# A mixture-of-experts kernel on one core: the head of x loaded by SyncE alone, in two pieces

## The chip, the cores and the metric

The kernel runs on one core of a Trainium2 chip. The core has five engines that run side by side and meet only through semaphores: TensorE (PE in the profile, PEld for its weight loads), VectorE (DVE), ScalarE (ACT), GpSimd (POOL) and SyncE (SP). Sixteen DMA engines move data between HBM and the on-chip memory (SBUF). A DMA is issued by SyncE, ScalarE or GpSimd; each of the three has a queue of its own on these sixteen engines: q1 is SyncE's, q10 ScalarE's, q0 GpSimd's. GpSimd's queue can also convert the data on the way, here from fp32 to bf16.

The metric is the device time of one execution in microseconds (us), the median of several runs. The span in a profile, from the first to the last instruction of the program, is a little shorter.

## The reference

Eight experts, each with its own 256 rows of x and its own two weight matrices:

```python
n_experts, capacity, hidden, expert_hidden = 8, 256, 512, 2048
h = np.matmul(x, w1)        # (8,256,512) x (8,512,2048)
h = np.maximum(h, 0)
out = np.matmul(h, w2)      # (8,256,2048) x (8,2048,512) -> (8,256,512)
```

Everything is fp32 in HBM. x has 4 MB, w1 and w2 have 32 MB each, and the output has 4 MB.

## The kernel before

**Layout.** x is seen as 128 partitions with R = 16 rows of 512 numbers each. w1 of an expert lies in SBUF as 128 partitions with all of its 2048 columns for K1 = 4 slices of the hidden dimension; w2 as 128 partitions with K2 = 16 slices. Both have NS = 4 slots, so expert e uses slot e mod 4. All weights become bf16 in the DMA.

**x comes in two parts.** The first HEAD = 6 of the 16 rows per partition come as fp32 into memory that belongs to the output (x_head, a part of out_sb), by two hardware-queue loads: rows 0 to 2 issued by SyncE and rows 3 to 5 issued by ScalarE (L137 to L141). Both raise the semaphore d_head. They are issued inside the Tile context; tc.close() and tc.compile() behind them (L142, L143) end that context with a barrier over all engines, and from there on the program is written by hand. The other ten rows are loaded by GpSimd behind that barrier (L158) straight into x_sb as bf16. x_sb is not memory of its own: it lies in slot 2 of w2_sb. VectorE waits for both head loads (d_head at 32) and casts the head to bf16 into x_sb in one instruction (L219).

**Transposes.** When the cast is done, the identity matrix is built and GpSimd's x load has landed, PE transposes x in 64 pieces of 128 by 128 (a loop over K1 = 4, 16 pieces each, matmuls recorded at the helper's line L280). VectorE and ScalarE copy the results from PSUM to xT (L211).

**Weights.** GpSimd issues twelve weight loads in one fixed order (L195): w1 then w2 for experts 0 and 1 together, then for 2 and 3, then w1 of 4 and 5, then w2 of 4, and so on, down to w2 of the last expert in two halves. Before some of them it waits until the slot is free: for w1 until the hidden matmuls of the expert four places earlier are done, for w2 until its output matmuls are. The load of w2 for experts 2 and 3 waits for all transposes, since x_sb lies in its place. q0 works these loads off in the order of issue.

**Who tells PE.** SyncE waits for each weight load to land, in that order (L148), and raises a counter that PE takes (helper `take`, L99). SyncE issues nothing else until the end, when it stores the last expert's output (L150).

**Compute.** Per expert PE makes 64 matmuls into h_ps in four groups; ScalarE applies the maximum with zero and writes hT (L244); then 32 matmuls into o_ps, which VectorE copies to out_sb (L230). The very last half is copied by ScalarE (L250). The outputs of the first seven experts go out in one large store by GpSimd (L198), queued behind the last weights.

Of the kernel before, what the change touches and what calls it, by code (L numbers as in the profile page):

```python
# [16 lines left out]
def kernel(  # L17
# [7 lines left out]
    nc = tc.nc  # L25
# [6 lines left out]

    R = E * C // P

    HEAD = 6

    NS = 4

# [94 lines left out]

    x_head = out_sb[:, :HEAD // MC].rearrange("p e m h -> p (e m h)")


    for queue, a, b in [(nc.sync, 0, HEAD // 2), (nc.scalar, HEAD // 2, HEAD)]:  # L137
        head = queue.dma_start(
            x_head[:, a * H:b * H], x_v[:, a * H:b * H]
        ).then_inc(d_head, 16)  # L140
        tc.info.no_tile_sem_insts.add(head.ins.name)  # L141
    tc.close()  # L142
    tc.compile()  # L143

    sp = nc.sync
    for i, (w, es, h, n) in enumerate(loads):
# [10 lines left out]
    pool = nc.gpsimd  # L157
    pool.dma_start(x_sb[:, HEAD * H:], x_v[:, HEAD * H:]).then_inc(d_pool, 16)  # L158
    pool.memset(identity[:], 0.0).then_inc(s_event)  # L159
# [58 lines left out]
    dve.wait_ge(d_head, 32)  # L218
    dve.tensor_copy(x_sb[:, :HEAD * H], x_head).then_inc(s_cast)  # L219
    dve.sem_inc(c_xt[0], 1)  # L220
# [259 lines left out]
```

## Time and profile before

| what | value |
|---|---|
| median of 3 runs | 179.18 us (179.18 to 179.47) |
| the profiled execution's own time | 179.18 us |
| its span | 177.9 us |
| busy share PE, ACT, DVE, POOL | 71%, 22%, 9%, 6% |
| share of the DMA engines' time by q0, q1, q10 | 97.1%, 2.1%, 1.1% |
| granted TensorE clock, mean | 0.942 |
| issue to landing of the head loads | 6.0 us (SyncE's), 6.9 us (ScalarE's) |
| issue to landing of GpSimd's x load | 10.5 us |

How to read the lines shown further down. In the busy line each digit is the busy share of one fortieth of the span in tenths. In a table of stretches each row gives the stretch, its length, the busy time and number of instructions of PE, PEld, DVE, ACT and POOL, the granted clock, the mean busy share of the DMA engines and the GB/s that they wrote; a packet counts where it starts, so shares of short stretches can pass 1. In the timeline a row gives start, duration, engine, line, operation, and in brackets how long the engine had been idle and what released it. "SPq" and the like are the engines' instruction queues, which handle semaphores and DMA issues.

### The profile page before, as it was taken

To read this page: it belongs to the slowest core of one execution; us is meant where nothing else is said; L and a number is where in the kernel's file an instruction comes from. 1 tells how busy PE (TensorE), PEld (TensorE's weight loads), DVE (VectorE), ACT (ScalarE), POOL (GpSimd) and SP (SyncE) were. 2 spreads that over 40 slices of the span, in tenths; PEclk is the share of its full clock that TensorE was granted. 3 is DMA by queue.
4 is the path that set the end of the run, shared out by engine and by line. 5 is a ranking of instruction groups with operands and counts; after the bars stand their busy time and mean duration, and the time that the engine had idled before them with its cause. 6 is when DMAs were issued, how large, how long until landed. Compare 5 with 4: busy or idle time off the path is not lost. (4 is left out here: it accounts for less than half of the span.)

```text
span 177.9 us, 2069 instructions
## 1 busy us (share of the span) xinstructions
PE 126.3 (71%) x824; PEld 89.5 (50%) x832; DVE 16.4 (9%) x20; ACT 38.7 (22%) x38; POOL 10.2 (6%) x21
## 2 busy tenths in 40 slices
PE   0008620794029999993059999999999999959980
PEld 0007510584014795692024794695596497449530
DVE  0214420000000200200000200200100020020010
ACT  2002420044000062054000062053044044006310
POOL 4300010000000002101000101100020000001000
PEclk9999999999558999999657999999999999999999
DMA  5999999989999989989999999999999999999998
GB/s 188 313 214 228 232 195 221 236 192 221 236 192 221 236 192 221 236 192 221 236 192 221 236 206 206 236 210 203 236 217 195 236 221 192 236 199 214 284 424 354
DMA packets 3888, 40.63 MB, mean 228 GB/s; under 512 B 304, under 2 KB 304, under 8 KB 1584
## 3 DMA queue, kind: packets, MB, share of 16 engines
q0 software_dynamic: 3456, 38.54, 97.1%
q1 hardware_dynamic: 288, 1.31, 2.1%
q10 hardware_dynamic: 144, 0.79, 1.1%
HBM read 71.30 MB, written 4.20 MB: 424 GB/s over the span
## 5 line engine op out<-in xcount | busy, mean ns | idle before, releaser
L280 PE MATMUL o_ps<-w_sb,hT 128*128 x248 | 59.7, 396 | 19.5 <-PEq L99 18.7
L280 PE MATMUL h_ps<-xT,w_sb 128*128 x512 | 60.7, 280 | 11.1 <-PEq L99 11.1
L280 PEld LDWEIGHTS h_ps<-xT,w_sb 128*128 x512 | 57.6, 145 | 15.1 <-issue 11.8
L244 ACT ACTIVATE hT<-h_ps 128x1024 bf16<-128x1024 f32 x32 | 32.8, 1024 | 109.6 <-PE h_ps L280 109.6
L280 PEld LDWEIGHTS o_ps<-w_sb,hT 128*128 128x128 bf16 x256 | 25.4, 101 | 51.1 <-issue 24.4
L230 DVE COPY out_sb<-o_ps 128x512 f32<-128x512 f32 x15 | 9.7, 687 | 139.7 <-PE o_ps L280 139.7
L280 PE MATMUL xt_ps<-identity,w_sb 128*128 128x128 bf16 x64 | 7.6, 310 | 15.7 <-PEq L99 15.7
L280 PEld LDWEIGHTS xt_ps<-identity,w_sb 128*128 x64 | 6.5, 144 | 16.5 <-issue 16.5
L195 POOL DMA_DIRECT2D w_sb<-in_w_dram x12 | 7.4, 616 | 104.4 <-PE h_ps L280 56.6
L211 ACT COPY xT<-xt_ps 128x1024 bf16<-128x1024 bf16 x4 | 4.0, 1012 | 17.0 <-PE xt_ps L280 17.0
L211 DVE COPY xT<-xt_ps 128x1024 bf16<-128x1024 bf16 x4 | 4.9, 1225 | 9.3 <-PE xt_ps L280 9.3
L198 POOL DMA_DIRECT2D out_dram<-out_sb x1 | 1.0, 964 | 33.0 <-DMA out_dram<-out_sb 33.0
L219 DVE CAST w_sb<-out_sb 128x3072 bf16<-128x3072 f32 x1 | 1.8, 1761 | 7.7 <-DMA out_sb<-in_x_dram 7.7
L250 ACT COPY out_sb<-o_ps 128x512 f32<-128x512 f32 x1 | 0.6, 586 | 5.9 <-PE o_ps L280 5.9
L211 ACT ACT_TABLE_LOAD x1 | 1.3, 1283 | 2.0 <-PEq L143 2.0
L186 POOL DMA_DIRECT2D out_dram<-out_sb x1 | 0.5, 512 | 14.7 <-DVEq L233 14.7
L158 POOL DMA_DIRECT2D w_sb<-in_x_dram x1 | 0.7, 682 | 2.0 <-POOLq L143 2.0
L162 POOL TENSOR_SCALAR_AFFINE_SELECT identity<-identity 128x128 bf16<-128x128 bf16 x1 | 0.3, 284 | 0.2 <-POOL identity L159 0.2
L159 POOL MEMSET identity<- 128x128 bf16 x1 | 0.2, 224 | 0.0
L464 POOL MEMSET const-float32-0.0<- 128x1 f32 x1 | 0.1, 93 | 0.2 <-issue 0.2
L464 POOL MEMSET const-bfloat16-1.0<- 128x1 bf16 x1 | 0.1, 96 | 0.0
L464 POOL MEMSET const-uint8-127<- 128x1 uint8 x1 | 0.1, 96 | 0.0
(1 smaller groups left out, 0.1 us busy)
## 6 DMA issues: line engine op xcount, KB each, us to landing
w_sb<-in_w_dram POOLq DMA_DIRECT2D x5, 4096.0 KB, 46.9
w_sb<-in_w_dram POOLq DMA_DIRECT2D x5, 2048.0 KB, 50.9
out_dram<-out_sb POOLq DMA_DIRECT2D x1, 3584.0 KB, 12.8
w_sb<-in_w_dram POOLq DMA_DIRECT2D x2, 1024.0 KB, 43.1
w_sb<-in_x_dram POOLq DMA_DIRECT2D x1, 1280.0 KB, 10.5
out_sb<-in_x_dram SPq DMA_DIRECT2D x1, 768.0 KB, 6.0
out_sb<-in_x_dram ACTq DMA_DIRECT2D x1, 768.0 KB, 6.9
out_dram<-out_sb SPq DMA_DIRECT2D x1, 512.0 KB, 4.6
```

Source lines behind the costliest of these rows:

```text
L158: pool.dma_start(x_sb[:, HEAD * H:], x_v[:, HEAD * H:]).then_inc(d_pool, 16)
L162: pool.affine_select(out=identity[:], in_=identity[:], compare_op=mybir.AluOpType.not_equal, fill=1.0, base=0, pattern=[[-1, P]], channel_ ...
L186: pool.dma_start(out_v[:16, 0, :16], out_sb[:16, 0, 0, :16]).then_inc(d_pool, 16)
L195: pool.dma_start(dst, src).then_inc(landed[i][0], 16)
L198: pool.dma_start(out_v[:, :E - 1, :], out_sb[:, :E - 1].rearrange("p e m h -> p e (m h)")).then_inc(d_pool, 16)
L211: return copy(xT[:, ko, m].rearrange("k (ep r2) -> k ep r2", r2=R // MC), xt_ps[m][:].rearrange("k r2 ep -> k ep r2"),)
L219: dve.tensor_copy(x_sb[:, :HEAD * H], x_head).then_inc(s_cast)
L230: cp = dve.tensor_copy(out_sb[:, e, m, :], o_ps[m][:])
L244: act.activation(hT[:, g * GJ:(g + 1) * GJ, :].rearrange("p a c -> p (a c)"), h_ps[g % UG][:], mybir.ActivationFunctionType.Relu,).then_in ...
L250: act.copy(out_sb[:, E - 1, 1, :], o_ps[1][:]).then_inc(v_last)
L280: return pe.add_instruction(inst)
L464: nc = _bacc.Bacc("TRN2", target_bir_lowering=False, num_devices=1)
```

## The change

Behind the change SyncE issues two loads for the head and ScalarE issues none. The first, four of the six rows, stands in the Tile context as before. The second, two rows, is SyncE's first instruction behind tc.close() and tc.compile(). Both raise d_head by 16, so the cast still waits for both (32). Rows, places in memory and everything behind them are unchanged.

```diff
-    HEAD = 6
+    FIRST, HEAD = 4, 6
...
-    for queue, a, b in [(nc.sync, 0, HEAD // 2), (nc.scalar, HEAD // 2, HEAD)]:
-        head = queue.dma_start(
+    def load_head(a, b):
+        return nc.sync.dma_start(
             x_head[:, a * H:b * H], x_v[:, a * H:b * H]
         ).then_inc(d_head, 16)
-        tc.info.no_tile_sem_insts.add(head.ins.name)
+
+    first = load_head(0, FIRST)
+    tc.info.no_tile_sem_insts.add(first.ins.name)
     tc.close()
     tc.compile()
+    load_head(FIRST, HEAD)
```

## The prediction

> **What bounds the kernel now.** First the whole profile: the busy line of the DMA engines, the queues' table, and the issues of the loads.
>
> ```profile
> span 177.9 us, 2069 instructions
> PE 126.3 (71%) x824; PEld 89.5 (50%) x832; DVE 16.4 (9%) x20; ACT 38.7 (22%) x38; POOL 10.2 (6%) x21
> ...
> DMA  5999999989999989989999999999999999999998
> q0 software_dynamic: 3456, 38.54, 97.1%
> q1 hardware_dynamic: 288, 1.31, 2.1%
> q10 hardware_dynamic: 144, 0.79, 1.1%
> HBM read 71.30 MB, written 4.20 MB: 424 GB/s over the span
> ```
>
> q0 is GpSimd's queue, q1 SyncE's, q10 ScalarE's. The digits stand at 8 or 9 in every slice but the first: the DMA engines have work from the second slice to the end, and 97.1% of their time goes to q0, the weights. PE, the busiest compute engine, has 71%. The profiled execution took 179.18 us, which is also the median of the three runs shown (179.18 to 179.47); 1.3 us of it lie around the span.
>
> Next the span cut into stretches. Columns: stretch, its length, busy time of PE, PEld, DVE, ACT and POOL, granted clock, DMA share, GB/s written.
>
> ```profile
> 1.50:3.00 1.50, 0.00 (x0) 0.00 (x0) 0.00 (x0) 1.02 (x1) 0.59 (x1) 1.00 0.78 152
> 3.00:6.00 3.00, 0.00 (x0) 0.00 (x0) 0.00 (x0) 0.27 (x1) 2.61 (x6) 1.00 1.01 422
> 6.00:12.50 6.50, 0.00 (x0) 0.00 (x0) 1.76 (x1) 0.00 (x0) 0.17 (x1) 1.00 1.14 247
> 12.50:32.40 19.90, 7.57 (x64) 6.52 (x64) 4.90 (x4) 4.05 (x4) 0.72 (x1) 1.00 1.00 213
> 32.40:51.80 19.40, 9.69 (x64) 8.33 (x65) 0.00 (x0) 4.10 (x4) 0.00 (x0) 0.81 1.01 216
> 90.50:158.20 67.70, 65.47 (x411) 44.09 (x416) 6.44 (x10) 16.39 (x16) 2.65 (x5) 0.96 1.01 216
> 167.90:175.50 7.60, 4.66 (x22) 1.91 (x20) 0.69 (x1) 0.59 (x1) 0.00 (x0) 1.00 1.03 423
> ```
>
> From 3 us on the DMA share is 1.00 or more. The written rate drops to about 215 GB/s only because the weights shrink from four bytes to two on the way: that is some 430 GB/s read, close to the 422 of the head. So nothing of the front part of the kernel has a price of its own except a moment in which the DMA engines stand still; whatever the order of the loads in the first 12.5 us, the same bytes pass before the first weights.
>
> The chain that ended last says how the end hangs on this stream, and the timeline shows the waits that it meets (in brackets the idle time before an instruction and what ended it).
>
> ```profile
> 158.30 7.31 PE h_ps L280 x64
> 172.60 0.59 ACT out_sb L250
> ```
>
> ```profile
> 32.46 0.83 PE L280 MATMUL h_ps<-xT,w_sb 128*128 x3 [9.20 <-PEq L99]
> 158.30 7.31 PE L280 MATMUL h_ps<-xT,w_sb 128*128 x64 [1.88 <-PEq L99]
> 173.21 0.35 SPq L150 DMA_DIRECT2D out_dram<-out_sb  x1
> ```
>
> L99 is the helper that takes a counter, here the one that SyncE raises when weights land: the last expert's w1 lands at 158.2, and PE, ScalarE and the last store follow. The other stores share the engines with it at 423 GB/s. A stream that is later by some time makes the end later by the same time, and PE's start at 32.46 waits for weights too.
>
> **The change part by part.** The pieces it touches:
>
> ```profile
> 0.74 0.38 SPq L138 DMA_DIRECT2D out_sb<-in_x_dram  x1
> 0.74 0.39 ACTq L138 DMA_DIRECT2D out_sb<-in_x_dram  x1
> 1.98 1.28 ACT L211 ACT_TABLE_LOAD   x1 [1.98 <-PEq L143]
> 2.40 0.68 POOL L158 DMA_DIRECT2D w_sb<-in_x_dram  x1 [1.96 <-POOLq L143]
> L143 SPq DRAIN  x3: 7/7/129, 1.2 to 1.6; - x3
> L143 ACTq DRAIN  x2: 8/81/154, 1.2 to 1.6; - x2
> L143 SPq EVENT_SEMAPHORE  x2: 17/17/17, 1.5 to 1.8; - x2
> ```
>
> *ScalarE's load goes* (0.39 us of issue). It stands ahead of the closing barrier of the Tile context (L143), which lets GpSimd go at 1.96. But SyncE's issue stands there too, started at the same 0.74 and took 0.38, and it stays; its first drain (129 ns at most against ScalarE's 154) ends 0.03 us before ScalarE's at best. So the barrier opens at most 0.03 us sooner. ScalarE's own work gains nothing: behind its table load it waits for PE's transposes, which start at 13.49 (row below). And even GpSimd's x load at 2.40 is queued behind the head's bytes, as the queues' table of the first 6 us shows:
>
> ```profile
> q1 hardware_dynamic: 128, 0.78, 40.9%
> q10 hardware_dynamic: 116, 0.71, 29.3%
> ```
>
> No packet of q0 moved before 6.0, although GpSimd's instruction was over at 3.1. Cost: 0.
>
> *SyncE's first load has four rows in place of three* (1024 KB in place of 768). Same issue count, same 0.38; the packets of a partition's rows get longer and not more. Cost 0 on the issue side.
>
> *SyncE's second load* (two rows, 512 KB) is one more issue on SyncE, 0.38 us, right behind the barrier's last semaphore on SP (1.8). What is queued behind it is the wait for the first weights, over at
>
> ```profile
> L148 SPq EVENT_SEMAPHORE  x2: 17/17/17, 32.3 to 51.7; - x2
> ```
>
> so 30 us cover it. When can its bytes flow? The first load's: the stretch 1.50:3.00 cut in 40 pieces of 0.0375 us, with its queues:
>
> ```profile
> GB/s 0 0 0 0 0 0 164 492 328 328 164 328 492 0 0 0 0 0 0 0 164 164 328 0 0 0 328 164 164 0 164 164 164 0 492 492 492 164 164 164
> q1 hardware_dynamic: 21, 0.13, 59.8%
> q10 hardware_dynamic: 16, 0.10, 18.5%
> ```
>
> The first piece with bytes is the seventh, at 1.73: 1.0 us behind the issue at 0.74. The second load, issued at about 1.85, is then ready at 2.85. The first load is done later: 0.23 MB by 3.0 (152 GB/s x 1.5 us), the rest of its 1.049 MB at 422 GB/s takes 1.94 us, so 4.94. Two us of margin, no hole. Then 0.524 MB at 422 take 1.24: the head's bytes end at 6.18. Today: 1.573 MB, (1.573 - 0.228) / 0.422 = 3.19, so 6.19. Cost 0.
>
> *What is late if the two rows mix with GpSimd's x load.* Both may then wait in their queues at 4.9. At worst the two rows end with that load, at 12.5 in place of 6.2, and land about 1 us later. The cast of the head (1.76 us at 7.68 now, in the 6.00:12.50 row) then ends at about 15.3, and the transposes, which start at
>
> ```profile
> 13.49 1.89 PE L280 MATMUL xt_ps<-identity,w_sb 128*128 128x128 bf16 x16 [13.49 <-PEq L99]
> ```
>
> slip by 1.8 us. PE's 9.20 us of idle time ahead of 32.46 cover this. GpSimd's w2 load that waits for the transposes,
>
> ```profile
> 3.98 2.18 POOL L195 DMA_DIRECT2D w_sb<-in_w_dram  x3 [0.15 <-issue]
> ...
> 23.56 0.72 POOL L195 DMA_DIRECT2D w_sb<-in_w_dram  x1 [17.39 <-PE xt_ps L280]
> ```
>
> goes out at 25.4 in place of 23.56. Three weight loads stand ahead of it on q0 since 3.98, and the second of them lands only at 51.7, so q0 stays full. Cost 0; it would begin to cost only when the transposes slipped by more than PE's idle 9.20.
>
> *One ring where there were two, while the stream starts up.* This the trace does not show. The stretch 1.50:3.00 carried 0.23 MB where 422 GB/s would have carried 0.63: 0.40 MB, or 0.96 us, are lost in the start-up. Lower end: all of that regained, -0.96, which the first piece's position already excludes in part (0.23 us pass before any byte): -0.7. Upper end: q1 carries no more than its own 0.13 MB there, and q10's 0.10 MB is missing: +0.24. The nearest row for one hardware queue alone is the last store:
>
> ```profile
> 176.20:177.20 1.00, 0.00 (x0) 0.00 (x0) 0.00 (x0) 0.00 (x0) 0.00 (x0) 1.00 0.95 389
> q1 hardware_dynamic: 99, 0.39, 94.6%
> ```
>
> In this microsecond q1, all but alone, kept the engines 95% busy: one ring is enough. I take 0.
>
> Sum: 179.18 + 0 (ScalarE's issue) + 0 (longer first load) + 0 (second load, covered by 2.1 us of bytes) + 0 (late cast, covered by 9.20) + 0 (start-up) = **179.2 us**.
>
> **The rivals.** *Slower: a hole behind the first load.* If SyncE's second load gets no bytes moving until the first has landed, and GpSimd's x load is truly not ready before 6.0 (no q0 packet is seen earlier), the DMA engines stand idle from 4.94 to 6.0, and the stream is late by 1.06 us: 179.18 + 1.06 = 180.2. It decides from the point where both are later than 4.94. For it: no row of before has two loads back to back on SyncE's queue. Against: twelve weight loads follow one another on q0 at a share of 1.00 to 1.01 without a hole, the x load's instruction was over at 3.1, and q0's packets begin just where the head's end, as those of a queue do that has been waiting. The Trainium skill speaks for this rival: its page "DMA: Bandwidth & Descriptors", section "Anatomy of one DMA — SWDGE (gpsimd) path", fits each DMA with about 2.0 us fixed plus its bytes at 436 GB/s, mostly for the receipt of the last byte. Paid in line behind the first load, that would make an estimate of 181.2. The trace of before does not agree on q0: where the next load is already queued, the share stays at 1.00 to 1.01 across the landings.
>
> *Faster: the start-up shrinks.* If the two rings hinder one another at the start (between 1.99 and 2.25 no packet starts, then both queues do), one ring could fill the engines earlier. Half of the 0.96 us regained gives 179.18 - 0.48 = 178.7. For it: that gap. Against: the gap can as well be the first packets' own way to HBM, which one ring has too.
>
> *Another null: the rows mix with the x load*, worked out above: same 179.2, but a later cast.
>
> **How the numbers follow.** No change, by either order, has 0.53: its own range is 178.9 to 179.5, the spread of the runs shown. The hole has 0.19 (179.6 to 180.2), the shorter start-up 0.16 (178.5 to 178.8); a start-up slower by up to 0.24 and what no row shows have the other 0.12, of which 0.06 stays within 0.2% (0.36 us, about what a measurement of this kernel can tell from no change), 0.04 is slower and 0.02 faster. Faster 0.18, same 0.59, slower 0.23. The range 178.6 to 180.2 holds the null, the hole up to its full price and most of the faster case, whose bound of -0.7 it leaves out.
>
> **What would show it.** Right: no q10 in the queues' table; q1 with about 1.57 MB in the first 6.2 us and a DMA share of about 1.0 over 3.0 to 6.0; the transposes within 2 us of 13.49; PE's first hidden matmul at 32.4 to 32.5 and the last expert's at 158.3. A hole shows as a share clearly under 1.0 between 4.9 and 6.0, with 158.3 moved by as much. A shorter start-up shows as more than 152 GB/s in 1.50:3.00, and both times earlier. The prediction is wrong if w1 of the last expert lands more than 0.4 us from 158.2, or if the time outside the span, 1.3 us, changes with ScalarE's queue gone, which no row can tell.

## The result, and the profile after

The changed kernel takes 180.23 us (median of 6 runs, 180.01 to 180.86) against 179.18 us of the kernel before (6 runs, 179.07 to 179.47). The ratio is 1.0059, with a 95% interval of 1.0046 to 1.0072: slower by 0.6%. The profiled execution took 180.51 us, 1.33 more than that of before, and its span grew by 1.3.

The page of the changed kernel, its lines of the span, the queues, the loads of x and the last store (KB and us from issue to landing):

```profile
span 179.2 us, 2069 instructions
...
q0 software_dynamic: 3456, 38.54, 96.6%
q1 hardware_dynamic: 432, 2.10, 3.2%
...
w_sb<-in_x_dram POOLq DMA_DIRECT2D x1, 1280.0 KB, 12.0
out_sb<-in_x_dram SPq DMA_DIRECT2D x1, 1024.0 KB, 4.7
out_sb<-in_x_dram SPq DMA_DIRECT2D x1, 512.0 KB, 12.3
out_dram<-out_sb SPq DMA_DIRECT2D x1, 512.0 KB, 3.0
```

q10 is gone and q1 carries all of the head. GpSimd's x load, untouched by the change, takes 12.0 us to land in place of 10.5. The second head load takes 12.3.

The timeline of the changed kernel:

```profile
0.74 1.49 SPq L137 DMA_DIRECT2D out_sb<-in_x_dram  x2
2.40 0.68 POOL L160 DMA_DIRECT2D w_sb<-in_x_dram  x1 [1.96 <-POOLq L144]
14.25 1.76 DVE L221 CAST w_sb<-out_sb 128x3072 bf16<-128x3072 f32 x1 [14.25 <-DMA out_sb<-in_x_dram]
16.46 1.89 PE L282 MATMUL xt_ps<-identity,w_sb 128*128 128x128 bf16 x16 [16.46 <-PEq L99]
26.54 0.72 POOL L197 DMA_DIRECT2D w_sb<-in_w_dram  x1 [20.37 <-PE xt_ps L282]
33.75 2.54 PE L282 MATMUL h_ps<-xT,w_sb 128*128 x11 [7.51 <-PEq L99]
159.62 2.75 PE L282 MATMUL h_ps<-xT,w_sb 128*128 x12 [2.67 <-PEq L99]
```

The first row joins both of SyncE's issues; it ends at 2.23, and the second began at 1.90. For the cast the kernel before had this row:

```profile
7.68 1.76 DVE L219 CAST w_sb<-out_sb 128x3072 bf16<-128x3072 f32 x1 [7.68 <-DMA out_sb<-in_x_dram]
```

The barrier opens when it did: GpSimd issues its x load at 2.40 in both. The cast moves from 7.68 to 14.25, the transposes from 13.49 to 16.46, and PE still sits idle for 7.51 us behind them before the first weights are there. But the weights are late: PE starts on them at 33.75 in place of 32.46, and on the last expert's at 159.62 in place of 158.30. The 1.3 us arise before the first weights have landed and stay the same to the end.

The stretches of the changed kernel, with the columns of the table shown for before:

```profile
1.50:3.00 1.50, 0.00 (x0) 0.00 (x0) 0.00 (x0) 1.02 (x1) 0.60 (x1) 1.00 0.78 202
3.00:6.00 3.00, 0.00 (x0) 0.00 (x0) 0.00 (x0) 0.26 (x1) 2.61 (x6) 1.00 1.02 388
6.00:12.50 6.50, 0.00 (x0) 0.00 (x0) 0.00 (x0) 0.00 (x0) 0.17 (x1) 1.00 1.04 214
158.20:167.90 9.70, 8.28 (x60) 7.42 (x61) 0.00 (x0) 3.07 (x3) 0.96 (x1) 0.82 1.01 213
```

The start-up is better than before (202 GB/s against 152). Then 3.00:6.00 moves 388 in place of 422, and 6.00:12.50 moves 214 in place of 247, with a DMA share of 1.0 all the time. There is no hole. The engines are busy and move less: single packets take longer, as the packet records of the next section show.

The same records show which engine counts. The 16 engines finish their parts of the first weights between 31.43 and 31.92 in the kernel before, and between 32.00 and 33.27 in the changed one: 0.62 us later on average, 1.35 for the last. In all twenty profiles of this document the span ends 145.9 to 146.0 us behind that last engine (146.2 in head4_only). So the time follows the slowest engine at the first weights.

The chain that ended last, for the end:

```profile
159.62 8.93 PE h_ps L282 x64
175.54 0.58 ACT out_sb L252
```

PE needs 8.93 us for the last hidden matmuls in place of 7.31, at a granted clock of 0.82 in 158.20:167.90. That is not what the change costs. The last store is issued later, but lands in 3.0 us in place of 4.6, and the span grows by the same 1.3 us that the weights are late. Two of the kernels below show the same pair without a difference in time: in sp4_sp2_inside the clock of this stretch is 0.82 and the last store takes 3.1 us, in sp4_act2_inside 1.00 and 4.6, and the span of both is 177.7.

### The profile page after: what moved, and what is told of

The parts are those of the page before. It is cut to its first block, busy times and chain, and to the rows that moved or that the text cites. A ratio compares the mean times of both kernels' runs of the same rounds, so it can differ in the third digit from the quotient of the medians.

```text
span 179.2 us, 2069 instructions
## 1 busy us (share of the span) xinstructions
PE 126.6 (71%) x824; PEld 89.6 (50%) x832; DVE 16.4 (9%) x20; ACT 38.7 (22%) x38; POOL 10.2 (6%) x21
## 5 line engine op out<-in xcount | busy, mean ns | idle before, releaser
L282 PE MATMUL h_ps<-xT,w_sb 128*128 x512 | 61.4, 282 | 10.2 <-PEq L99 10.2
## 6 DMA issues: line engine op xcount, KB each, us to landing
out_dram<-out_sb POOLq DMA_DIRECT2D x1, 3584.0 KB, 12.9
out_sb<-in_x_dram SPq DMA_DIRECT2D x1, 512.0 KB, 12.3
```

Source lines behind the costliest of these rows:

```text
L282: return pe.add_instruction(inst)
```

## The experiments

Each changes something about how the loads are issued. In the cuts of their code `...` stands for lines left out. Where load_head has four arguments, the first is the engine that issues, and True marks a load that stands in the Tile context. "First weights" is SyncE's first wait for a landing; it stands at 32.3 us in the kernel before and at 33.6 in the changed kernel:

```profile
L150 SPq EVENT_SEMAPHORE  x12: 17/17/17, 33.6 to 169.2; - x12
```

### Place, ring or sizes

Three things change together: the second load's place (behind the closing), its ring, that is, the queue (SyncE's twice), and the sizes (four and two rows). Four kernels set them apart.

```diff
 # sp4_sp2_inside: both of SyncE's loads in the Tile context
+    load_head(nc.sync, 0, FIRST, True)
+    load_head(nc.sync, FIRST, HEAD, True)
     tc.close()
     tc.compile()
-    load_head(FIRST, HEAD)
...
```

> Both of SyncE's loads stand in the Tile context, so the second is issued some 0.8 us sooner; sizes and ring are those of the changed kernel. Theory P (the place behind the closing makes the second load late on some DMA engines, GpSimd's x load cuts in there, and the slowest engine sets when the first weights land): 179.2 us, first weights landed at about 32.3, head landed before 8. Theory R (two loads in one ring do it): 180.2, first weights at 33.6. Theory S (loads of 4 and 2 rows, with 8 KB and 4 KB pieces, do it): 180.2.

Measured: 179.08 us, ratio 0.9987 [0.9976, 0.9999], first weights at 32.1.

```diff
 # sp4_act2_inside
+    load_head(nc.sync, 0, FIRST, True)
+    load_head(nc.scalar, FIRST, HEAD, True)
     tc.close()
     tc.compile()
-    load_head(FIRST, HEAD)
...
```

> The kernel before with 4 rows on SyncE and 2 on ScalarE, both in the Tile context: the sizes alone. Theory S: 180.2 us, first weights landed at 33.6. Theories P and R: 179.2 and 32.3.

Measured: 179.14 us, ratio 0.9992 [0.9980, 1.0005], first weights at 32.1. The sizes cost nothing.

```diff
 # sp4_act2_behind
...
     tc.compile()
-    load_head(FIRST, HEAD)
+    load_head(nc.scalar, FIRST, HEAD, False)
```

> 4 rows on SyncE in the Tile context, 2 rows on ScalarE behind the closing: the place and the sizes of the changed kernel, but two rings. Theories P and S: 180.2 us, first weights landed at 33.6, head landed at about 14. Theory R: 179.2 and 32.3, head landed before 8.

Measured: 180.43 us, ratio 1.0070 [1.0053, 1.0087], first weights at 33.4, cast at 13.30. Two rings do not help.

```diff
 # sp3_sp3_behind
-    first = load_head(0, FIRST)
+    load_head(nc.sync, 0, HEAD // 2, True)
     tc.close()
     tc.compile()
-    load_head(FIRST, HEAD)
+    load_head(nc.sync, HEAD // 2, HEAD, False)
...
```

> SyncE loads three rows in the Tile context and three behind the closing: place and ring of the changed kernel, sizes of the kernel before. Theories P and R: 180.2 us or more, since the first load is shorter and ends at about 4.3 us. Theory S: 179.2.

Measured: 181.05 us, ratio 1.0088 [1.0063, 1.0113], first weights at 34.2. So neither the ring nor the sizes alone cost anything; the three slow kernels share the place behind the closing, where the second load is issued at 1.9 us (inside, SyncE issues it at 1.17). Sizes matter in that a shorter first load makes it worse. With both loads inside, the barrier also opens later (GpSimd issues its x load at 2.88 in place of 2.40); that this is not what helps is shown further down, by pool_x_later, where a later x load does not help, and by sp5_sp1_behind, which is clean with the x load at 2.41.

The kernel with both loads inside has the sizes and the ring of the changed kernel, so the two can be laid side by side, but for its x load, issued 0.48 us later. What the queues carried from 4.8 to 6.0 us and from 6.5 to 8.5 us (packets, MB, share of the 16 engines' time), first with both loads inside:

```profile
DMA packets 136, 0.53 MB, mean 439 GB/s; under 512 B 13, under 2 KB 13, under 8 KB 132
q1 hardware_dynamic: 133, 0.50, 100.8%
...
DMA packets 45, 0.46 MB, mean 230 GB/s; under 512 B 0, under 2 KB 0, under 8 KB 0
q0 software_dynamic: 45, 0.46, 109.4%
```

and in the changed kernel:

```profile
DMA packets 113, 0.42 MB, mean 348 GB/s; under 512 B 14, under 2 KB 14, under 8 KB 111
q1 hardware_dynamic: 111, 0.40, 95.8%
...
DMA packets 39, 0.35 MB, mean 175 GB/s; under 512 B 0, under 2 KB 0, under 8 KB 8
q0 software_dynamic: 31, 0.32, 88.1%
q1 hardware_dynamic: 8, 0.03, 4.3%
```

In the first stretch the busy time is nearly the same, with a fifth fewer bytes; in the second, 31 packets of the x load start in place of 45. In the packet records a 4 KB piece of the second load takes 0.16 us, but five of them near 5 us take 0.3 to 1.1; a piece of the x load takes 0.77 us, but many near 7 us take 1.0 to 1.2. Added up over the 16 engines, the packets that are more than 0.1 us too long account for 0.60 us per engine, 0.16 of it in the second load and 0.45 in the x load, and the bytes moved up to 14 us are 0.62 us behind those of before. With both loads inside the same count gives 0.01.

Not every engine is hit alike. Twelve of the 16 finish the second load at 6.1 to 6.3 us, the other four, on which it shares the engine with the x load, at 10.8 to 13.9. A load has landed when the last of the 16 engines has: GpSimd's x load, issued at 2.40, lands at 2.40 + 12.0 = 14.4 in place of 2.40 + 10.5 = 12.9. So the mean is 0.62 us late and the first weights 1.3.

### GpSimd's descriptors, or a load into a running stream

```diff
 # pool_x_later: a fill of 128x1024 fp32 in an unused part of out_sb first
...
+    pool.memset(out_sb[:, E - 1], 0.0).then_inc(s_late)
+    pool.wait_ge(s_late, 1)
     pool.dma_start(x_sb[:, HEAD * H:], ...)
...
 # pool_w_later: three such fills ahead of the weight loads
```

> The changed kernel, but GpSimd first fills a part of out_sb that nobody reads before it is overwritten (estimated at 1.1 us from the 0.22 us for 128 columns), so that its x load and its weight loads are issued about 1.1 us later. Theory G (SyncE's second load is held up because GpSimd writes the descriptors of its own loads at the same time): the second load of the head gets through, the head's bytes end near 6.2, first weights land near 32.3, 179.2 us, unless the x load itself now comes too late. Theory B (a hardware-queue load that is issued while the DMA engines already move data comes through slowly, whoever else issues): the stream is disturbed between 4.9 and 8 us as in the changed kernel, 180.2 us.

Measured: 180.32 us, ratio 1.0063 [1.0046, 1.0080], first weights at 33.5. The x load was issued at 3.17. Here the head landed early (cast at 7.50), and now it is the x load's first packets that are stretched, by up to 1.1 us each. The loss is as large, but it has moved to the other load. So the second load gets through as theory G had it, and the time is as theory B had it.

> The changed kernel, but GpSimd makes three such fills between the identity and the first weight load, so that the x load stays where it was and the three weight loads are issued near 7 us in place of 4 to 6.2. Theory G in the form that the weight loads' descriptors do it: undisturbed from 4.9 to 6.5 and about 179.2 us. Theory G in the form that the x load's descriptors (2.4 to 3.1 us) do it, and theory B: 180.2.

Measured: 180.10 us, ratio 1.0053 [1.0037, 1.0070], first weights at 33.2, with the weight loads issued from 7.05 on. Their descriptors have no part in it.

```diff
 # head4_only: no second load, GpSimd loads twelve rows
-    FIRST, HEAD = 4, 6
+    HEAD = 4
...
-    load_head(FIRST, HEAD)
...
-    dve.wait_ge(d_head, 32)
+    dve.wait_ge(d_head, 16)
```

> The second load is left out: SyncE loads four rows in the Tile context, GpSimd the other twelve (1536 KB). If the disturbance belongs to the second hardware-queue load, this is as fast as before or a little faster, 179.0 to 179.2 us, with q0's first packets at about 4.9. If GpSimd's x load is itself not ready before 6 us, a hole from 4.9 to 6 shows and the time is about 180.2.

Measured: 180.14 us, ratio 1.0057 [1.0040, 1.0074], first weights at 32.6. What q0 and q1 carried from 4.4 to 6.0 us:

```profile
q0 software_dynamic: 30, 0.37, 113.6%
q1 hardware_dynamic: 31, 0.12, 18.7%
```

q0 starts as soon as the four rows are through (first packet at 4.7), so GpSimd's x load is ready long before the 6.0 at which it is first seen in the kernel before. Packets are stretched by 0.10 us per engine, less than in the changed kernel, although the x load is only 2.3 us old when it starts. The first weights are only 0.3 us late, yet the runs are 1.0 us slower, of which the profiled execution, the fastest of the four (179.73), shows 0.55; where the rest lies in the others isn't known. Neither of the two forecasts holds: there is no hole, and leaving the second load out does not bring the time of before back.

```diff
 # both_behind: both of SyncE's loads behind the closing
-    first = load_head(0, FIRST)
     tc.close()
     tc.compile()
+    load_head(0, FIRST)
     load_head(FIRST, HEAD)
```

> Both of SyncE's loads stand behind the closing, one right after the other (about 1.9 and 2.3 us), so that the stream starts about 1.16 us later than in the kernel before, which costs 1.16 by itself: 180.3. Theory B: the second is issued before the DMA engines move data, so nothing is added: 180.3, and the stretch in which the head moves runs at about 420 GB/s. Theory G: the second load is generated beside GpSimd's x load, the stream is disturbed as well: 181 or more.

Measured: 179.79 us, ratio 1.0032 [1.0020, 1.0043], first weights at 32.9. With no DMA to issue, the closing itself is over sooner (loads at 1.39 and 1.82), so the start is late by 0.65 us and not by the 1.16 that was expected; 0.40 us of that is left by 4 us, and the stream loses only 0.15 more. The second load's first packet is at 5.3, 3.5 us behind its issue. Stretches of this kernel:

```profile
3.50:6.00 2.50, 0.00 (x0) 0.00 (x0) 0.00 (x0) 0.00 (x0) 2.16 (x3) 1.00 1.09 427
```

427 GB/s: as theory B has it, no disturbance worth the name.

```diff
 # pool_x_after_head
+    pool.wait_ge(d_head, 32)
     pool.dma_start(x_sb[:, HEAD * H:], ...)
```

> The changed kernel, but GpSimd issues its x load only when the whole head has landed, so that the second load has the DMA engines for itself and a hole opens between the head and the x load. The time itself is of no use (about 182 us with a hole of some 2 to 3 us). Theory B (a hardware-queue load issued while data already moves is held up by itself): the head's last bytes move at clearly less than 420 GB/s and the second load lands later than 7.6. Theory M (it is the meeting of the second load with the x load on the engines): the second load moves at about 420 GB/s, ends at 6.2 and lands at about 7.2, and the x load behind it is undisturbed too.

Measured: 183.5 us in one run, with the hole that was expected. The second load alone on the engines still has five stretched packets (0.3 to 0.5 us), but lands by 7.15. The x load behind the hole:

```profile
7.43 1.60 POOL L161 DMA_DIRECT2D w_sb<-in_x_dram  x1 [6.98 <-DMA out_sb<-in_x_dram]
DMA packets 16, 0.16 MB, mean 109 GB/s; under 512 B 0, under 2 KB 0, under 8 KB 0
```

The second line is for 9.5 to 11.0 us: one packet per engine in that time, stretched by 0.4 to 1.0 us, starting 2.3 us behind the beginning of the issue, which itself took 1.60 us here in place of 0.68. Neither theory said this: a load that starts on idle engines is slow in its first packets, on q0 here as on q1 at the kernel's start, where the first sixteen 8 KB pieces take 0.4 to 1.05 us each and later ones 0.31.

```diff
 # before_plus_early, before_plus_late: the kernel before and a third load
     sp = nc.sync
...
+    sp.wait_ge(d_head, 32)          # only in before_plus_late
+    sp.dma_start(out_sb[:, 4]..., x_v[:, 4 * H:6 * H]).then_inc(d_extra, 16)
...
+                dve.wait_ge(d_extra, 16)   # before VectorE writes there
```

> The kernel before plus a third load: SyncE reads two rows of x once more, behind the closing, into a part of out_sb that is not yet in use (VectorE waits for it before it writes there). Its 0.524 MB cost 1.24 us at 422 GB/s. Theories B and M: on top of that the x load is stretched and the first weights land later by about 1 us: 181.2 or more, first weights at 34.5. If only a load that the cast waits for matters: 180.4, first weights at 33.5.

Measured: 180.54 us, ratio 1.0073 [1.0054, 1.0092], first weights at 33.6, 1.3 us later: the price of the bytes and no more. Behind the start-up not one packet is stretched, though the load was issued at 1.90 into a running stream, as in the changed kernel; its own first packet is at 6.0, 4.1 us behind the issue. Theory B falls in its general form, and so does M.

> The same third load, but issued when the head has landed (about 7.7 us), into the middle of GpSimd's x load. 1.24 us for its bytes. Theory B in its general form (any hardware-queue load issued into a running stream disturbs it): about 1 us on top, first weights at 34.5, 181.4 us. If the disturbance belongs to the meeting of two loads that both have just been issued: 180.4, first weights at 33.5.

Measured: 180.49 us, ratio 1.0071 [1.0054, 1.0087], first weights at 33.6. Again only the bytes.

```diff
 # sp6_inside: all six rows in one load
-    FIRST, HEAD = 4, 6
+    HEAD = 6
...
-    load_head(FIRST, HEAD)
...
-    dve.wait_ge(d_head, 32)
+    dve.wait_ge(d_head, 16)
```

> All six rows in one load by SyncE in the Tile context, none by ScalarE. No load is issued behind the closing on a hardware queue, so by every theory left this is undisturbed: 179.0 to 179.2 us, first weights at 32.1 to 32.3.

Measured: 179.09 us, ratio 0.9995 [0.9985, 1.0005], first weights at 32.3, and behind the start-up only three packets are more than 0.1 us too long (by 0.12 at most). ScalarE's load is not needed, and taking it away brings nothing.

### How old a load is when its turn comes

What the clean runs with a load in the Tile context share is that the bytes issued there last longer. That can be tried directly.

```diff
 # sp5_sp1_behind: FIRST, HEAD = 5, 6     sp2_sp4_behind: FIRST, HEAD = 2, 6
 # sp6_sp2_behind: FIRST, HEAD = 6, 8 (GpSimd loads eight rows)
 # sp6_sp2_later: the same, and
+    nc.sync.wait_ge(s_event, 2)     # GpSimd's identity
     load_head(FIRST, HEAD)
```

> Five rows in the Tile context, one row behind the closing. The first load's bytes end at about 5.5 us, so the second, issued at 1.9, has a lead of 3.6. Theory L (the lead counts, 3.6 us are enough): 179.1 to 179.3 us, first weights landed at 32.2 to 32.4. Theory A (0.63 us per row of the second load): 179.8, 32.9.

Measured: 179.45 us, ratio 1.0014 [0.9999, 1.0030], first weights at 32.2. One packet of the second load is 0.19 us too long, none of the x load.

> Six rows in the Tile context and two behind the closing (8 rows by SyncE, 8 by GpSimd). The second load is the one of the changed kernel in size and time of issue, but its turn comes at about 6.1 us, a lead of 4.2. Theory L: 179.1 to 179.3 us, first weights at 32.2 to 32.4. Theory A: 180.4, 33.6.

Measured: 179.20 us, ratio 1.0003 [0.9992, 1.0014], first weights at 32.2, no packet of the second load or of the x load stretched. This is the second load of the changed kernel, same size, same place, same issue at 1.90. Its turn comes later, and GpSimd has eight rows in place of ten. Theory A (a price per row) falls.

> As sp6_sp2_behind, but SyncE issues the second load only when GpSimd's identity is finished (about 3.9 us), so that its lead is 2.2 us. Theory L: disturbed again, as much as the kernel with three rows and three rows, first weights at 33.6 to 34.2, 180.4 to 181. Theory A: as sp6_sp2_behind. If the cover of x load and weights already queued on GpSimd's queue fills in, it is clean: 179.2.

Measured: 179.22 us, ratio 1.0001 [0.9992, 1.0011], first weights at 32.3, the third of the cases named; theory L's own forecast (33.6 to 34.2) missed. The x load was ready and went first, and the two rows came in between its packets from 7.4 us on, when they were 3.5 us old and not 2.2:

```profile
0.74 3.44 SPq L137 DMA_DIRECT2D out_sb<-in_x_dram  x2
15.40 2.29 DVE L222 CAST w_sb<-out_sb 128x4096 bf16<-128x4096 f32 x1 [15.40 <-DMA out_sb<-in_x_dram]
```

(The first row joins both issues: the second ends at 4.18.) The cast is later here than in the changed kernel, and it costs nothing.

> Two rows in the Tile context and four behind the closing; the first load's bytes end at about 3.6 us, a lead of 1.7. Theory L: the worst of the row, first weights later than 34.2 and more than 181 us. Theory A: four rows at 0.63, 34.8 and 181.7.

Measured: 181.72 us, ratio 1.0144 [1.0126, 1.0162], first weights at 34.7, the worst of the row as both theories said.

The kernels in one row, by the age of the second load (the time since its issue, the lead of the expectations) when its first packet starts:

| kernel | first packet of the second load at | age of the second load | first weights at |
|---|---|---|---|
| sp2_sp4_behind | 3.5 | 1.6 | 34.7 |
| sp3_sp3_behind | 4.1 | 2.2 | 34.2 |
| changed kernel | 4.8 | 2.9 | 33.6 |
| sp4_sp2_inside | 4.7 | 3.5 | 32.1 |
| sp5_sp1_behind | 5.4 | 3.5 | 32.2 |
| sp6_sp2_behind | 5.9 | 4.0 | 32.2 |

(These are times of the first engine; the others reach this point within 0.3 to 0.5 us. With both loads inside the second is issued at 1.17.) The other kernels with a second load issued by SyncE or ScalarE fit: sp4_act2_behind, pool_w_later and pool_x_later have ages of 2.7 to 2.8 and first weights at 33.2 to 33.5; both_behind, with 3.5, loses only 0.15 us beyond its late start. GpSimd's x load does not line up by its age: it is clean at 3.1 us in sp4_sp2_inside, stretched by 0.09 us per engine at 2.3 in head4_only, by 0.63 at 2.7 in pool_x_later and by 0.45 at 3.3 in the changed kernel.

A last kernel was to say whether it is this age (L) or simply that the bytes of the Tile context last until about 5.5 us (C).

```diff
 # sp4_sp2_later: the changed kernel, and
+    nc.sync.wait_ge(s_event, 2)
     load_head(FIRST, HEAD)
```

> The changed kernel, but SyncE waits for GpSimd's identity (about 3.9 us) before it issues the second load. Theory L (fresh packets cost): GpSimd's x load, issued at 2.4, takes the DMA engines at 4.8, the two rows come in between its packets from 7 us on, no longer fresh; the stream is nearly as in the kernel without the second load: first weights at 32.3 to 32.9, 179.2 to 179.8 us, faster than the changed kernel although a load is issued later. Theory C (the first load must last until 5.5 us): as the changed kernel or worse, 33.6 and 180.2 us.

Measured: 180.00 us, ratio 1.0042 [1.0019, 1.0065]; the ten runs spread from 179.16 to 181.40, far more than those of any other kernel here. In the profiled one (180.43) the x load takes over at 4.7, 2.3 us old, with most packets in order (the bytes are 0.14 us behind in place of 0.62), but two of the 16 engines finish it 0.6 and 1.3 us behind all others, and the first weights land at 33.5. That is near C's forecast, but the ten runs cover the times of both forecasts. It fits L only if the x load, too, is too young at its turn; the two are not separated.

> The kernel with both of SyncE's loads in the Tile context once more, with more rounds. By the first comparison 0.13% faster than the kernel before; the first weights landed 0.15 us sooner. Expected: a ratio of 0.9985 to 0.9998.

Measured: 179.13 us, ratio 1.0002 [0.9990, 1.0014]. The small gain of the first comparison isn't confirmed: no version tried beats the kernel before.

## Why the prediction was wrong, point by point

**ScalarE's load goes, at 0.** Right. GpSimd's x load is issued at 2.40 as before, and one load by SyncE alone (sp6_inside) gives 179.09.

**The late cast, at 0.** Right. The two rows mixed with the x load on four of the 16 engines, the cast slipped by 6.6 us and the transposes by 3.0 (1.8 were forecast), and PE's idle time covered it; sp6_sp2_later has a still later cast and no loss.

**The start-up, at 0.** Slightly pessimistic: the stretch 1.50:3.00 moves 202 GB/s in place of 152, which is 0.18 us ahead; it was inside the stated bounds and was lost again.

**The second load, covered by 2.1 us of bytes, at 0.** This is the step that failed. It took the 1.0 us from the first load's issue to its first byte as the time after which a load is ready, and so saw the second load waiting since 2.85 when its turn came at 4.9. The turn came at 4.8, and the load did start there, but packets of it and of the x load behind it were stretched, 0.60 us per engine, and the slowest engine was 1.35 us late at the first weights. SyncE's second loads ran clean or nearly so when they were 3.5 us old at their turn, those of 2.9 us and less did not; that it is the age itself is not shown (see sp4_sp2_later). A hint stood in a row that was shown: in the stretch 1.50:3.00 the first packets of the first load, too, moved far below the later rate, and the forecast booked this as a price of the kernel's start, paid once.

**What bounds the kernel.** That the stream of loads bounds it was right, and is the reason why the loss shows in full: nothing takes it up again between 33 and 160 us. What was concluded from it was not, that nothing in the front part has a price except a moment in which the DMA engines stand still. The engines did not stand still, and the loss came all the same: 388 GB/s in place of 422 at a share of 1.02.

**The rival "a hole behind the first load".** Its place was right, and its price (1.06 us, 180.2) is the measured 180.23 within 0.03, but that is luck, for its mechanism was wrong: its condition that the x load be not ready before 6.0 is refuted by head4_only, the second load's bytes moved from 4.8 on, before the first had landed at 5.4, and the DMA share shows no idle engines. The estimate of 181.2 that the fixed part of the Trainium skill's page "DMA: Bandwidth & Descriptors" (section "Anatomy of one DMA — SWDGE (gpsimd) path") would have given is not reached either. That page of the Trainium skill fits its figure to loads issued by GpSimd, and the second load is SyncE's. In before_plus_early a third load by SyncE costs its bytes alone (1.3 us, where 1.24 were worked out from 422 GB/s).

**The range.** 178.6 to 180.2 left the result out by 0.03 us: the hole's price was taken as its upper end without anything for the engine that comes last.

## What to carry to other kernels

In a kernel bound by its DMA stream, work out how long ago the next load was issued when its turn comes. Here a load by SyncE or ScalarE ran nearly clean from 3.5 us on, and at 2.9 us and less it did not; whether the age does it or the length of the load ahead is open, and for GpSimd's load no such bound shows. Measure readiness on a load that takes over from another one, not on the first byte of a load into idle engines. And judge such a handover by its slowest engine: landing needs all sixteen.

## What the runs showed that was not expected

- The second load did not leave the engines idle at its turn; it kept them busy for longer. The DMA share was 1.0 at 388 GB/s as at 422, so the share alone would have called this stream full.
- What makes the first packets slow isn't shown. That the x load, 3.3 us old or more, is stretched as well behind the slow second load (near 7 us, on most engines at once) isn't explained by its age, and it is the larger part of the loss.
- A load that is ready can wait behind others for long: in the kernel before, q0's packets begin at 6.0, and in head4_only an x load of twelve rows, issued at the same 2.4, starts at 4.7.
- A closing of the Tile context with no DMA issued inside opens the barrier 0.5 us sooner (GpSimd's x load at 1.90 in place of 2.40 in both_behind), and with two issued inside by SyncE it opens 0.5 us later (2.88 in sp4_sp2_inside).
